# A gated-convolution and RG-LRU layer on one core: the 512-column moving operands of TensorE stored even columns first and read in pairs

## The chip, the cores and the metric

The kernel runs on one core of one Trainium2 chip. The metric is the device time of one execution in microseconds (us); lower is better. Before the change three timed runs gave 851.17, 851.32 and 853.02 us, a median of 851.32. The trace that is read here is a further execution that took 851.45 us; its first and last instruction lie 849.7 us apart (the span).

## The reference, cut to what matters

One layer acts on 512 latent tokens and 256 context tokens of width 2048, all in float32:

```
mod_lat = silu(c) @ w_ada + b_ada                 # shift, scale, gate; the same for c_ctx
hl = rmsnorm(x)   * (1 + scale_l) + shift_l       # 512 latent tokens
hc = rmsnorm(ctx) * (1 + scale_c) + shift_c       # 256 context tokens
b, c, u, g, v, q = split(h @ w_in)                # w_in: 2048 x 6144; context needs v alone
ya = b * conv3(c * u) * silu(g)                   # head group A
xb = conv4(v) + bias                              # head group B
a, bt = lru_coeffs(xb)                            # two directions, 16 block-diagonal heads
yb = (scan_fwd + scan_bwd) * silu(q)              # latent scans start from the context's state
out = x + gate_l * (concat(ya, yb) @ w_out)       # w_out: 2048 x 2048
return rmsnorm(out) * final_g
```

## The kernel before, in words

The host lays the inputs out: x is handed over transposed, as 16 tiles of 128 channels by 512 tokens (`xt`), w_in as tiles of 128 rows whose columns are the weights of one or several output tiles, w_out as 32 pieces of 128 rows by two times 512 columns (`wout`).

Large products run in float32r, one pass over the array, and three of them make one product of nearly float32 accuracy. Each operand is split into a high part, rounded to float32r by ScalarE, and a low part, the difference, by VectorE (`split`, lines 70 to 75; `make_h`, lines 250 to 254; `y_split`, lines 573 to 578). `mm3` (lines 77 to 80) then issues high times high, low times high and high times low into one accumulator in PSUM. In a matmul one operand is stationary: 128 columns of it are loaded into the array first. The other, the moving operand, streams through it column by column, here 512 at a time, or 256 for the context.

The work goes in three phases, and TensorE's instruction order is the order of the program text:

- Phase A (lines 222 to 346). Sums of squares over the 16 x tiles give rinvB, the inverse norm of each token, spread over the partitions. Then, for each of the 16 slices k of the 2048 channels: the adaLN products of that slice (`ada`, 64 small float32 matmuls of 64 columns by 32), the normalised latent tile h (`h_lat`), and seven output tiles of w_in (`main_a`), whose seven accumulators stay open over the whole loop. h is the moving operand, tokens along its columns.
- Phase B (lines 581 to 624). The other 41 output tiles of w_in come as 82 pieces of 1024 columns, each half of one tile's reduction: 8 slices, three matmuls of 512 latent columns each. The v tiles take the context's 256 columns too. Between the pieces run the convolutions, the gates and the RG-LRU of one of eight channel blocks at a time (`l_prep`, `l_gate`, `l_exp`, `l_mul`, `l_scan`), spread over steps by a table (`bg`, `mid`). VectorE also sums up the gate products of adaLN (`gt_acc`).
- Phase D (lines 680 to 734). The product with w_out, 8 pieces for each of four column blocks c of 512. Here the weights are the moving operand (lines 705 to 707), and the split y tiles, 128 tokens at a time, are stationary. Four token blocks t give four accumulators. VectorE adds the residual (`d_add`), ScalarE sums squares (`d_sq`), and `fin0` to `fin2` normalise and store. In the first three column blocks the adaLN gate is multiplied onto the product; in the last one (c == 3) `split_piece` (lines 314 to 321) multiplies it onto the 1024 raw weights before they are split.

Weights come through five raw buffers and three split ones. One DMA queue, SyncE's, issues all loads; a piece is loaded three steps and split two steps ahead of its use.

Nothing is computed along the columns of h before the matmuls that mixes them: the norm's square sums, rinvB and h keep whatever order of tokens x arrives in. The columns of PSUM that a matmul writes are in the order in which its moving columns are read.

Of the kernel before, what the change touches and what calls it, by code (L numbers as in the profile page):

```python
# [10 lines left out]
ALU = mybir.AluOpType  # L11
# [4 lines left out]
KT = D // 128  # L16
T = 512
# [26 lines left out]
N_D = 32  # L44
# [5 lines left out]
def tile_hybrid_layer(ctx, tc, xt, ct, xn, wada, wgt, bgt, wa_, wbc, wout, lruw, par, ident, fg, out):  # L50
    nc = tc.nc
# [8 lines left out]
    hl = s_lat.enter_context(p_lat)  # L60
# [9 lines left out]
    def split(raw, n=1024):  # L70
        hi = stage.tile([128, 1024], F32R, name="whi", bufs=3)
        lo = stage.tile([128, 1024], F32R, name="wlo", bufs=3)
        nc.scalar.copy(hi[:, :n], raw[:, :n])  # L73
        nc.vector.tensor_tensor(lo[:, :n], raw[:, :n], hi[:, :n].bitcast(F32), op=ALU.subtract)  # L74
        return hi, lo

    def mm3(acc, wh, wl, h, n, first, last, **kw):
        nc.tensor.matmul(acc, wh, h[0][:, :n], start=first, stop=False, **kw)  # L78
        nc.tensor.matmul(acc, wl, h[0][:, :n], start=False, stop=False, **kw)  # L79
        nc.tensor.matmul(acc, wh, h[1][:, :n], start=False, stop=last, **kw)  # L80


    pt = const.tile([128, NP], F32, name="pt")
# [7 lines left out]
    for k in range(KT):  # L91
        t = hl.tile([128, T], F32, name="xhi", bufs=17)
# [70 lines left out]
    acc = [pa.tile([128, 512], F32, name="bacc") for i in range(NA - 2)]  # L163
# [19 lines left out]
    gq = [None]  # L183
# [52 lines left out]
    for j in range(4):  # L236
        nc.tensor.matmul(acc[5][:, 2 * j:2 * j + 2], ssum[:, 128 * j:128 * j + 128], cmean[:, 0:2],
                         start=True, stop=True, skip_group_check=True)
# [57 lines left out]
    def main_a(k, j):  # L296
        hi, lo = wsp["a", k]
        s = slice(128 * j, 128 * j + 128)
        mm3(acc[j], hi[:, s], lo[:, s], hlat[k], T, k == 0, k == KT - 1)
# [9 lines left out]
    def load_piece(s):  # L309
        t = raw_tile()  # L310
        nc.sync.dma_start(t, piece_src(s))
        rawq[s] = t

    def split_piece(s):
        raw = rawq.pop(s)
        c = (s - N_BC) // 8
        if c == 3:
            r3 = raw.rearrange("p (k n) -> p k n", k=2)
            g = gq[0][:, None, 512 * c:512 * c + 512].to_broadcast([128, 2, 512])
            nc.vector.tensor_tensor(r3, r3, g, op=ALU.mult)  # L320
        wsp[s] = split(raw)

    h_lat(0)
# [193 lines left out]
    for m in range(NM):  # L517
        b = S_C0 + 7 * m
# [46 lines left out]
    accs = {}  # L565
# [7 lines left out]
    def y_split(pool, k):  # L573
        hi = pool.tile([128, T], F32R, name="yhi")
        lo = pool.tile([128, T], F32R, name="ylo")
        nc.scalar.copy(hi, y_src(k))
        nc.vector.tensor_tensor(lo, y_src(k), hi.bitcast(F32), op=ALU.subtract)
        yhl[k] = (hi, lo)

    load_piece(2)  # L580
    for s in range(N_BC):
        ti, half = divmod(s, 2)
        n, m = BC_TILES[ti]
# [8 lines left out]
        if s + 2 < NS:  # L592
            split_piece(s + 2)
        for _ in range(min(len(evq), 4 if s == 0 else 2)):
            evq.pop(0)()
        hi, lo = wsp.pop(s)
# [4 lines left out]
        for k in range(8):  # L601
# [3 lines left out]
            kk = 8 * half + k  # L605
            w = slice(128 * k, 128 * k + 128)
            mm3(accs[ti][0], hi[:, w], lo[:, w], hlat[kk], T, kk == 0, kk == KT - 1)
        if n == "v":
            for k in range(8):
                kk = 8 * half + k  # L610
                w = slice(128 * k, 128 * k + 128)
# [20 lines left out]
    def d_add(c, t, ps):  # L632
        s = slice(512 * c, 512 * c + 512)
        if c < 3:
            g = dr.tile([128, 512], F32, name="dg", bufs=1)
            nc.vector.tensor_tensor(g, gq[0][:, s], ps, op=ALU.mult)  # L636
            ps = g
        nc.vector.tensor_tensor(xr[t][:, s], xr[t][:, s], ps, op=ALU.add)

    def d_sq(c, t):  # L640
        s = slice(512 * c, 512 * c + 512)
        sqd = dr.tile([128, 512], F32, name="dsq", bufs=1)
        nc.scalar.activation(sqd, xr[t][:, s], AF.Square, accum_out=ss[:, t, c:c + 1])
        if c < 3:
            nc.gpsimd.tensor_tensor(xr[t][:, s], xr[t][:, s], fgb[:, s], op=ALU.mult)

    def d_ev(c, t, ps):
        d_add(c, t, ps)
        d_sq(c, t)
# [30 lines left out]
    for q in range(N_D):  # L680
        s = N_BC + q
        c, kp = divmod(q, 8)
        if s + 3 < NS:
            load_piece(s + 3)
        if s + 2 < NS:
            split_piece(s + 2)
        if kp == 0:
            if pend is not None:
                for t in range(2):
                    d_ev(pend[0], t, pend[1][t])  # L690
            accs = [pa.tile([128, 512], F32, name="bacc") for _ in range(2 if c == 1 else 4)]
            if c == 1:
                pp = pa.tile([128, 2, 512], F32, name="plru", bufs=1)
                accs += [pp[:, 0, :], pp[:, 1, :]]
        if q < 5:
            nc.sync.dma_start(*((xr[q], xn[q]) if q < 4 else (fgb, fg)))
        hi, lo = wsp.pop(s)

        def dmm(t, kp, hi, lo):
            for i in range(2):  # L700
                kk = 2 * kp + i
                yh, yl = yhl[kk]
                ts = slice(128 * t, 128 * t + 128)
                w = slice(512 * i, 512 * i + 512)
                nc.tensor.matmul(accs[t], yh[:, ts], hi[:, w], start=kk == 0, stop=False)  # L705
                nc.tensor.matmul(accs[t], yh[:, ts], lo[:, w], start=False, stop=False)  # L706
                nc.tensor.matmul(accs[t], yl[:, ts], hi[:, w], start=False, stop=kk == KT - 1)  # L707

        if c == 3 and kp >= 5:
            tailw[kp] = (hi, lo)  # L710
            if kp == 7:
                for t in range(4):
                    for kq in range(5, 8):
                        dmm(t, kq, *tailw[kq])
                    d_add(3, t, accs[t])
                    d_sq(3, t)
                    fin1(t)
                    fin2(t)
        else:
            for t in range(4):  # L720
                dmm(t, kp, hi, lo)
        if c == 0:
            for k in range(2 * kp + 6, 2 * kp + 8):
                if k < KT:
                    y_split(dp1[0] if k < 8 else dp, k)
        if pend is not None and kp < 2:
            d_ev(pend[0], kp + 2, pend[1][kp + 2])
            if kp == 1:
                pend = None
        if c == 3 and kp == 4:  # L730
            for t in range(4):
                fin0(t)
        if kp == 7:
            pend = (c, accs)


def _layout(np, x, c, ctx, c_ctx, norm_g, w_ada, b_ada, w_in, w_conv_a, w_conv_b, b_conv_b,
            lru_wa, lru_ba, lru_wx, lru_bx, lru_lambda, w_out, final_g):
    ca = np.ascontiguousarray
    a = {}  # L740
    a["xt"] = ca(x[0].T.reshape(KT, 128, T))
    a["ct"] = ca(ctx[0].T.reshape(KT, 128, TC))
    a["xn"] = ca(x[0].reshape(4, 128, D))
    w = w_ada[0]

    shp, scp, gtp = w[:, :D], w[:, D:2 * D], w[:, 2 * D:]
    g = np.stack([scp.reshape(2, 8, 128, KT, 4, 32), shp.reshape(2, 8, 128, KT, 4, 32)], axis=5)
    a["wada"] = ca(g.transpose(3, 0, 2, 1, 4, 5, 6).reshape(KT, 2, 128, 2048))
    a["wgt"] = ca(gtp.reshape(KT, 128, 2, 1024).transpose(0, 2, 1, 3).reshape(2 * KT, 128, 1024))
    a["bgt"] = ca(b_ada[0, 2 * D:].reshape(1, D))  # L750
    wi = w_in[0].reshape(KT, 128, 48, 128)
    a["wa_"] = ca(wi[:, :, [W_OFF[n] + m for n, m in A_TILES], :].reshape(KT, 128, NA * 128))
    wb = wi[:, :, [W_OFF[n] + m for n, m in BC_TILES], :].reshape(2, 8, 128, len(BC_TILES), 128)
    a["wbc"] = ca(wb.transpose(3, 0, 2, 1, 4).reshape(N_BC, 128, 1024))
    wo = w_out[0].reshape(8, 2, 128, 4, 512)
    a["wout"] = ca(wo.transpose(3, 0, 2, 1, 4).reshape(N_D, 128, 1024))

    wl = np.stack([lru_wa[0], lru_wx[0]], axis=3).reshape(2, NM, 2, 64, 128)
    wl = wl.transpose(1, 3, 0, 2, 4).reshape(NM, 64, 512)
    a["lruw"] = ca(np.concatenate([wl, wl], axis=1))  # L760
    col = lambda v: v.reshape(-1, 128).T
    gb = np.concatenate([lru_ba[0].reshape(2, NM, 2, 64), lru_bx[0].reshape(2, NM, 2, 64)], axis=3)
    parts = {
        "ng": col(norm_g[0]), "bsc": col(b_ada[0, D:2 * D]), "bsh": col(b_ada[0, :D]), "c": col(c[0]),
        "cc": col(c_ctx), "wca": w_conv_a[0].reshape(3, NM, 128).transpose(2, 1, 0).reshape(128, 24),
        "wcb": w_conv_b[0].reshape(4, NM, 128).transpose(2, 1, 0).reshape(128, 32), "bcb": col(b_conv_b[0]),
        "gb": gb.transpose(3, 1, 0, 2).reshape(128, 32),
        "lam": lru_lambda[0].reshape(2, NM, 128).transpose(2, 1, 0).reshape(128, 16),
    }
    a["par"] = ca(np.concatenate([parts[n] for n, _ in PCOLS], axis=1))  # L770
    a["ident"] = np.eye(128, dtype=np.float32)
    a["fg"] = ca(np.broadcast_to(final_g, (128, D)))
    return a
# [19 lines left out]
```

## Time and profile before

| | before |
|---|---|
| median of three timed runs | 851.32 us |
| profiled execution | 851.45 us |
| its span | 849.7 us |
| TensorE matmul busy | 825.0 us (97%) |
| weight loads busy (beside matmuls) | 678.4 us (80%) |
| VectorE, ScalarE, GpSimd busy | 478.5, 365.5, 89.3 us |
| mean granted TensorE clock | 0.995 of full speed |

In the rows, PE is TensorE's matmuls, PEld its weight loads, DVE VectorE, ACT ScalarE, POOL GpSimd, SP SyncE; L78 is line 78 of the kernel. A name such as `bacc<-xhi,whi` reads: written tile, then moving operand, then stationary operand. Matmuls are pipelined, and the length shown for one contains the time its last column needs to come out of the array; what one matmul costs in a stream is the distance from its start to the next one's. A float32 product that is not float32r appears as two records, one for each of its passes.

### The profile page before, as it was taken

Reading aid. Unit: us, or ns where it says so; the run is one execution under the profiler, and the core shown is the slowest. Engines: PE = TensorE matmul, PEld = TensorE weight load, DVE = VectorE, ACT = ScalarE, POOL = GpSimd, SP = SyncE. Lnnn points to the kernel's source line nnn. Section 1 sums busy time; section 2 is a strip of 40 time slices with the busy share of each in tenths; the row PEclk is TensorE's granted clock in tenths of the full one; section 3 lists DMA queues with packets and bytes.
Section 4 is the critical chain, followed back from the end, with each engine's and each line's share of the span. In section 5 each row is a group of like instructions: output and inputs, shape, how many; then the busy total and the mean of one; then the engine's idle time right before and its main releaser. Section 6 shows DMA issues by size and latency. Waiting matters only on the chain.

```text
span 849.7 us, 13489 instructions
## 1 busy us (share of the span) xinstructions
PE 825.0 (97%) x5712; PEld 678.4 (80%) x5712; DVE 478.5 (56%) x639; ACT 365.5 (43%) x454; POOL 89.3 (11%) x64
## 2 busy tenths in 40 slices
PE   7899999999999999999999999999999999999995
PEld 2687787888888888878888888887878888888784
DVE  3644344884653564585848566764556734243565
ACT  4322124541010125757584857565847522222334
POOL 0000004300000000202020202120202002020200
PEclk9999999999999999999999999999999999999998
DMA  9989996433333234342535353433224732323205
GB/s 343 417 337 358 335 373 206 150 103 121 100 100 100 81 106 160 121 163 100 185 98 164 120 186 103 161 124 115 88 93 147 289 100 87 112 76 123 75 0 198
DMA packets 36494, 136.31 MB, mean 160 GB/s; under 512 B 4049, under 2 KB 6353, under 8 KB 31697
## 3 DMA queue, kind: packets, MB, share of 16 engines
q1 hardware_dynamic: 36434, 135.45, 46.1%
q8 instruction: 45, 0.74, 0.4%
q14 instruction: 15, 0.12, 0.0%
HBM read 131.24 MB, written 4.19 MB: 159 GB/s over the span
## 4 chain that ended last, share of the span: by engine, by line
PE 90%; DVE 4%; DMA 2%; ACT 2%; issue 1%; POOL 0%; SPq 0%; ACTq 0%; DVEq 0%; POOLq 0%
PE bacc L78 21%; PE bacc L79 20%; PE bacc L80 20%; PE bacc L705 6%; PE bacc L707 6%; PE bacc L706 6%; PE bacc L208 4%; DMA xhi<-in_xt 1%; DMA rada<-in_wada 1%; PE plru L450 1%; PE plru L707 1%; PE plru L706 1%; PE plru L78 1%; PE plru L79 1%; PE plru L80 1%
## 5 line engine op out<-in xcount | busy, mean ns | idle before, releaser
L74 DVE TENSOR_TENSOR wlo<-raw,whi 128x1024 fp32r<-128x1024 f32 (+1 forms) x130 | 160.3, 1237 | 242.7 <-ACT whi L73 241.3
L78 PE MATMUL bacc<-xhi,whi 128*128 128x512 f32 x736 | 291.1, 395 | 2.9 <-issue 1.6
L79 PE MATMUL bacc<-xhi,wlo 128*128 128x512 f32 x736 | 287.8, 391 | 2.6 <-issue 2.0
L80 PE MATMUL bacc<-hlo,whi 128*128 128x512 f32 x736 | 287.7, 391 | 1.4 <-issue 1.4
L73 ACT CAST whi<-raw 128x1024 fp32r<-128x1024 f32 (+1 forms) x130 | 134.3, 1035 | 236.2 <-PE bacc L80 126.0
L78 PEld LDWEIGHTS bacc<-xhi,whi 128*128 128x128 f32 x736 | 138.5, 188 | 33.2 <-issue 2.1
L80 PEld LDWEIGHTS bacc<-hlo,whi 128*128 128x128 f32 x736 | 138.5, 188 | 32.0 <-issue 2.2
L79 PEld LDWEIGHTS bacc<-xhi,wlo 128*128 128x128 f32 x736 | 138.6, 188 | 31.2 <-issue 2.3
L705 PE MATMUL bacc<-whi,yhi 128*128 128x512 f32 x224 | 87.3, 390 | 0.3 <-DVE dg L636 0.3
L707 PE MATMUL bacc<-whi,ylo 128*128 128x512 f32 x224 | 87.2, 389 | 0.0
L706 PE MATMUL bacc<-wlo,yhi 128*128 128x512 f32 x224 | 87.1, 389 | 0.0
L460 POOL TENSOR_TENSOR li<-li,xb 128x768 f32<-128x768 f32 x16 | 30.9, 1933 | 395.6 <-ACT li L457 395.6
L705 PEld LDWEIGHTS bacc<-whi,yhi 128*128 128x128 f32 x224 | 42.0, 188 | 9.6 <-DVE dg L636 1.0
L456 ACT ACTIVATE lr<-plru,pt 64x768 f32<-64x768 f32 x32 | 28.7, 898 | 48.3 <-PE plru L453 41.3
L252 ACT ACTIVATE xhi<-xhi,sh 128x512 fp32r<-128x512 f32 x16 | 11.6, 724 | 87.9 <-DVE xhi L251 87.9
L706 PEld LDWEIGHTS bacc<-wlo,yhi 128*128 128x128 f32 x224 | 42.0, 188 | 8.7
L707 PEld LDWEIGHTS bacc<-whi,ylo 128*128 128x128 f32 x224 | 42.1, 188 | 8.7
L500 DVE SCALAR_TENSOR_TENSOR gacc<-raw,cs,gacc 128x1024 f32<-128x1024 f32 x32 | 42.5, 1328 | 0.1
L79 PE MATMUL bacc<-xchi,wlo 128*128 128x256 f32 x128 | 36.2, 283 | 0.0
L80 PE MATMUL bacc<-hclo,whi 128*128 128x256 f32 x128 | 36.2, 283 | 0.0
L78 PE MATMUL bacc<-xchi,whi 128*128 128x256 f32 x128 | 36.1, 282 | 0.0
L208 PEld LDWEIGHTS bacc<-rada,cs 128*32 128x32 f32 x2048 | 29.5, 110 | 6.7 <-issue 6.4
(158 smaller groups left out, 864.0 us busy)
## 6 DMA issues: line engine op xcount, KB each, us to landing
raw<-in_wbc SPq DMA_DIRECT2D x82, 512.0 KB, 3.5
rada<-in_wada SPq DMA_DIRECT2D x32, 1024.0 KB, 8.0
raw<-in_wgt SPq DMA_DIRECT2D x32, 512.0 KB, 4.4
raw<-in_wout SPq DMA_DIRECT2D x32, 512.0 KB, 3.5
raw<-in_wa_ SPq DMA_DIRECT2D x16, 448.0 KB, 9.4
xhi<-in_xt SPq DMA_DIRECT2D x16, 256.0 KB, 4.8
xr<-in_xn SPq DMA_DIRECT2D x4, 1024.0 KB, 4.9
xchi<-in_ct SPq DMA_DIRECT2D x16, 128.0 KB, 4.4
```

What stands on the lines that cost most here:

```text
L73: nc.scalar.copy(hi[:, :n], raw[:, :n])
L74: nc.vector.tensor_tensor(lo[:, :n], raw[:, :n], hi[:, :n].bitcast(F32), op=ALU.subtract)
L78: nc.tensor.matmul(acc, wh, h[0][:, :n], start=first, stop=False, **kw)
L79: nc.tensor.matmul(acc, wl, h[0][:, :n], start=False, stop=False, **kw)
L80: nc.tensor.matmul(acc, wh, h[1][:, :n], start=False, stop=last, **kw)
L208: nc.tensor.matmul(o[32 * q:32 * q + 32], cs[:, 8 * p + j, :], r[:, j, q, :], start=p + j == 0, stop=p + j == 8, skip_group_check=True)
L456: nc.scalar.activation(lru["r", d][o], pf[0:64, :TA], AF.Sigmoid, bias=b[0:64])
L460: nc.gpsimd.tensor_tensor(lru["i", d], lru["i", d], xb[m], op=ALU.mult)
L500: nc.vector.scalar_tensor_tensor(gacc[:, s], gtq.pop(i), cs[:, k, 0:1], gacc[:, s], op0=ALU.mult, op1=ALU.add)
L705: nc.tensor.matmul(accs[t], yh[:, ts], hi[:, w], start=kk == 0, stop=False)
L706: nc.tensor.matmul(accs[t], yh[:, ts], lo[:, w], start=False, stop=False)
L707: nc.tensor.matmul(accs[t], yl[:, ts], hi[:, w], start=False, stop=kk == KT - 1)
```

## The change

The host stores the 512 columns of every x tile, and of each 512-column half of a w_out piece, even columns first: 0, 2, 4, ..., 510, 1, 3, ..., 511. `pairs` gives the matmul a view of such an operand that reads one column of the first half, one of the second, and so on, which is the original order 0, 1, 2, 3, ... Consecutive columns that the matmul reads are thus 256 elements (1024 bytes) apart in SBUF, where they were adjacent. The results in PSUM have the order they had. The multiplication of the gate onto the last eight w_out pieces becomes two VectorE instructions of 512 columns, which read the gate with a step of two elements, in place of one of 1024. The context's matmuls of 256 columns, the adaLN products and the RG-LRU's gate products stay as they are.

```diff
--- before.py
+++ after.py
@@ -74,10 +74,15 @@
         nc.vector.tensor_tensor(lo[:, :n], raw[:, :n], hi[:, :n].bitcast(F32), op=ALU.subtract)
         return hi, lo
 
-    def mm3(acc, wh, wl, h, n, first, last, **kw):
-        nc.tensor.matmul(acc, wh, h[0][:, :n], start=first, stop=False, **kw)
-        nc.tensor.matmul(acc, wl, h[0][:, :n], start=False, stop=False, **kw)
-        nc.tensor.matmul(acc, wh, h[1][:, :n], start=False, stop=last, **kw)
+    def pairs(ap):
+
+        return ap.rearrange("p (a b) -> p b a", a=2)
+
+    def mm3(acc, wh, wl, h, n, first, last):
+        hh, hl = (pairs(t) if n == T else t[:, :n] for t in h)
+        nc.tensor.matmul(acc, wh, hh, start=first, stop=False)
+        nc.tensor.matmul(acc, wl, hh, start=False, stop=False)
+        nc.tensor.matmul(acc, wh, hl, start=False, stop=last)
 
 
     pt = const.tile([128, NP], F32, name="pt")
@@ -315,9 +320,10 @@
         raw = rawq.pop(s)
         c = (s - N_BC) // 8
         if c == 3:
-            r3 = raw.rearrange("p (k n) -> p k n", k=2)
-            g = gq[0][:, None, 512 * c:512 * c + 512].to_broadcast([128, 2, 512])
-            nc.vector.tensor_tensor(r3, r3, g, op=ALU.mult)
+            g = gq[0][:, 512 * c:512 * c + 512].rearrange("p (b a) -> p a b", a=2)
+            for r in (raw[:, :512], raw[:, 512:]):
+                r = r.rearrange("p (a b) -> p a b", a=2)
+                nc.vector.tensor_tensor(r, r, g, op=ALU.mult)
         wsp[s] = split(raw)
 
     h_lat(0)
@@ -702,9 +708,10 @@
                 yh, yl = yhl[kk]
                 ts = slice(128 * t, 128 * t + 128)
                 w = slice(512 * i, 512 * i + 512)
-                nc.tensor.matmul(accs[t], yh[:, ts], hi[:, w], start=kk == 0, stop=False)
-                nc.tensor.matmul(accs[t], yh[:, ts], lo[:, w], start=False, stop=False)
-                nc.tensor.matmul(accs[t], yl[:, ts], hi[:, w], start=False, stop=kk == KT - 1)
+                wh, wl = pairs(hi[:, w]), pairs(lo[:, w])
+                nc.tensor.matmul(accs[t], yh[:, ts], wh, start=kk == 0, stop=False)
+                nc.tensor.matmul(accs[t], yh[:, ts], wl, start=False, stop=False)
+                nc.tensor.matmul(accs[t], yl[:, ts], wh, start=False, stop=kk == KT - 1)
 
         if c == 3 and kp >= 5:
             tailw[kp] = (hi, lo)
@@ -738,7 +745,9 @@
             lru_wa, lru_ba, lru_wx, lru_bx, lru_lambda, w_out, final_g):
     ca = np.ascontiguousarray
     a = {}
-    a["xt"] = ca(x[0].T.reshape(KT, 128, T))
+
+    even = lambda v: ca(v.reshape(*v.shape[:-1], -1, 2).swapaxes(-1, -2)).reshape(v.shape)
+    a["xt"] = even(x[0].T.reshape(KT, 128, T))
     a["ct"] = ca(ctx[0].T.reshape(KT, 128, TC))
     a["xn"] = ca(x[0].reshape(4, 128, D))
     w = w_ada[0]
@@ -753,7 +762,7 @@
     wb = wi[:, :, [W_OFF[n] + m for n, m in BC_TILES], :].reshape(2, 8, 128, len(BC_TILES), 128)
     a["wbc"] = ca(wb.transpose(3, 0, 2, 1, 4).reshape(N_BC, 128, 1024))
     wo = w_out[0].reshape(8, 2, 128, 4, 512)
-    a["wout"] = ca(wo.transpose(3, 0, 2, 1, 4).reshape(N_D, 128, 1024))
+    a["wout"] = even(wo.transpose(3, 0, 2, 1, 4)).reshape(N_D, 128, 1024)
 
     wl = np.stack([lru_wa[0], lru_wx[0]], axis=3).reshape(2, NM, 2, 64, 128)
     wl = wl.transpose(1, 3, 0, 2, 4).reshape(NM, 64, 512)
```

## Rows read from the trace of the kernel before

**Rows 1.** The page: busy time by engine, granted clock in 40 slices, chain by engine

```profile
PE 825.0 (97%) x5712; PEld 678.4 (80%) x5712; DVE 478.5 (56%) x639; ACT 365.5 (43%) x454; POOL 89.3 (11%) x64
...
PEclk9999999999999999999999999999999999999998
...
PE 90%; DVE 4%; DMA 2%; ACT 2%; issue 1%; POOL 0%; SPq 0%; ACTq 0%; DVEq 0%; POOLq 0%
```

**Rows 2.** Groups by line, forms kept apart: names, shapes, xcount | busy us, mean ns

```profile
L78 PE MATMUL bacc<-xhi,whi 128*128 128x512 f32 x736 | 291.1, 395 | 2.9 <-issue 1.6 <-ACT whi L73 1.3
...
L705 PE MATMUL bacc<-whi,yhi 128*128 128x512 f32 x224 | 87.3, 390 | 0.3 <-DVE dg L636 0.3
...
L78 PE MATMUL plru<-xhi,whi 128*128 128x512 f32 x32 | 12.5, 389 | 0.0
...
L705 PE MATMUL plru<-whi,yhi 128*128 128x512 f32 x32 | 12.4, 389 | 0.0
```

**Rows 3.** Timeline of TensorE at the end of phase D: start us, length us, line, operation

```profile
831.62 0.39 PE L706 MATMUL bacc<-wlo,yhi 128*128 128x512 f32 x1
...
840.69 0.39 PE L707 MATMUL bacc<-whi,ylo 128*128 128x512 f32 x1
```

**Rows 4.** Timeline of TensorE in phase B, context columns of a v tile

```profile
282.00 0.28 PE L79 MATMUL bacc<-xchi,wlo 128*128 128x256 f32 x1
...
283.92 0.28 PE L80 MATMUL bacc<-hclo,whi 128*128 128x256 f32 x1
```

**Rows 5.** Timeline of TensorE in phase A, after a wait

```profile
38.96 0.59 PE L79 MATMUL bacc<-xhi,wlo 128*128 128x512 f32 x1 [1.96 <-issue]
...
39.77 0.63 PE L78 MATMUL bacc<-xhi,whi 128*128 128x512 f32 x1
...
41.48 0.63 PE L79 MATMUL bacc<-xhi,wlo 128*128 128x512 f32 x1
...
42.27 0.39 PE L78 MATMUL plru<-xhi,whi 128*128 128x512 f32 x1
```

**Rows 6.** Windows: us, busy of PE, PEld, DVE, ACT, POOL (xcount), PEclk, DMA, GB/s

```profile
39.00:42.00 3.00, 3.00 (x8) 2.32 (x8) 2.13 (x5) 1.55 (x2) 0.00 (x0) 0.50 1.03 424
...
580.00:583.00 3.00, 3.00 (x12) 1.79 (x11) 0.01 (x1) 1.10 (x2) 1.70 (x1) 1.00 0.87 273
```

**Rows 7.** Chain of waits, in order of time: start us, us, what

```profile
580.73 1.72 PE bacc L505 x4
```

**Rows 8.** TensorE's waits: waited for: us in total, times, longest us

```profile
PE bacc L79 <- issue: 2.0, 1, 2.0
PE plru L450 <- ACT li L457: 1.7, 2, 1.2
...
PE bacc L78 <- issue: 1.6, 1, 1.6
PE bacc L80 <- issue: 1.4, 1, 1.4
...
PE bacc L208 <- issue: 0.9, 1, 0.9
...
PE bacc L705 <- DVE dg L636: 0.3, 1, 0.3
```

**Rows 9.** VectorE's groups by line: columns as in rows 2

```profile
L636 DVE TENSOR_TENSOR dg<-gacc,bacc 128x512 f32<-128x512 f32 x10 | 6.8, 683 | 0.2
...
L153 DVE TENSOR_TENSOR w<-w,w 128x16 f32<-128x16 f32 x7 | 1.2, 175 | 0.2
...
L132 DVE TENSOR_TENSOR cs<-pt,sg 128x16 f32<-128x16 f32 x2 | 0.3, 184 | 2.1 <-ACT sg L130 2.1
```

**Rows 10.** Timeline of VectorE in phase D, between two w_out pieces

```profile
788.30 1.22 DVE L320 TENSOR_TENSOR raw<-raw,gacc 128x1024 f32<-128x1024 f32 x1
792.59 1.22 DVE L74 TENSOR_TENSOR wlo<-raw,whi 128x1024 fp32r<-128x1024 f32 x1 [3.08 <-ACT whi L73]
```

## The prediction

> **What bounds the kernel now.** I read the page first. TensorE is busy for 97% of the span, its granted clock reads 9 or more tenths in every slice but the last, and 90% of the chain that ended last runs over TensorE [rows 1]. So what one matmul costs in a stream decides, and VectorE (56%) and ScalarE (43%) lie beside it.
>
> The groups by line, forms kept apart, give the number of matmuls that the change touches [rows 2]. L78, L79 and L80 each have 736 of 512 columns into `bacc` and 32 into `plru`; L705, L706 and L707 have 224 and 32 each. That is 3 x 768 + 3 x 256 = 3072.
>
> The timeline gives their price. Between the starts at 831.62 and 840.69 lie 40 matmuls of 512 columns: 9.07 / 40 = 0.2267 us [rows 3]. Between 282.00 and 283.92 lie 16 of 256 columns: 0.120 us [rows 4]. The difference, 256 columns in 106.7 ns, is 2.4 columns per ns, one for each tick of the clock's upper level of 2.4 GHz. So 512 columns take 213.3 ns, and 13.3 ns per matmul are fixed. 3072 x 0.2267 = 696 us of the 849.7 us span are such matmuls.
>
> Two more rows say something on that fixed part. After a wait of 1.96 us the granted clock was 0.50 (the 1.2 GHz level), and the matmuls of 512 columns came every (41.48 - 39.77) / 4 = 0.4275 us [rows 5, 6]. That is 512 columns at 1.2 per ns (426.7 ns) with nothing fixed. And at a granted clock of 1.00 the four float32 passes of L505, also with 512 contiguous columns, took 1.72 us, 0.43 each [rows 6, 7]: two ticks per column, again with 3 ns left at most. The fixed 13.3 ns show only where a column is taken at each tick of 2.4 GHz. My reading, which no row proves: whatever brings the moving columns out of SBUF has no slack at that rate, and ample slack at half of it. Then anything that makes the bringing slower is paid in full.
>
> **The change part by part.** (1) In 3072 matmuls consecutive columns lie 1024 bytes apart, not 4. No row of TensorE shows a moving operand read in this way, so I bound it. The low end is below zero: the fixed 13.3 ns vanish, which would be -13.3 x 3072 = -40.9 us. For the high end the nearest row is on VectorE: L132 writes 16 elements 128 bytes apart in 184 ns, L153 writes 16 adjacent ones in 175 [rows 9], so 9 / 16 = 0.56 ns more per element. VectorE's own pace is (683 - 175) / (512 - 16) = 1.02 ns per column [rows 9], so a far element takes about 1.59 ns, 1.55 times a near one. Carried over as a time, 512 columns take 813 ns and a matmul 813 + 13.3 = 826: +600 ns, 3072 x 0.600 = +1842 us. Carried over as a factor, 213.3 x 1.55 = 331, and +117 ns each, +360 us.
>
> Between these I take one column per two ticks: two adjacent columns can come in one access, two far ones can't. Its row is TensorE's own half-rate stream, 427 to 430 ns for 512 columns [rows 5, 7]. A matmul then costs 426.7 + 13.3 = 440 ns, +213.3 ns, and 3072 x 0.2133 = +655.4 us. I keep the fixed part in it, since the reading would again be what is late; without it the sum would be 41 us less.
>
> [...]
>
> (2) What the added time hides. TensorE's waits in the loops are 2.0 + 1.7 + 1.6 + 1.4 + 0.9 + 0.3 = 7.9 us [rows 8]; they end with loads and with work on ScalarE and VectorE. With matmuls twice as long all these come early against TensorE, so the waits go. The stretch at half clock followed the longest of them; its seven matmuls at 0.43 in place of 0.23 us are another 1.4 us. Together -9.3 us. A lower clock, should the slower stream bring one, would cost little: at 1.2 GHz a column takes the 0.83 ns that it would cost anyhow [rows 5].
>
> (3) The gate on the last eight w_out pieces: one VectorE instruction of 1.22 us [rows 10] becomes two. By L636, which also multiplies 512 columns, they take 2 x 0.683 = 1.37 us [rows 9], 0.15 more; if the gate's step of two elements costs like the far elements of L132, 2 x (0.683 + 512 x 0.00056) = 1.94, 0.72 more. Per piece VectorE then sits idle for 3.08 us [rows 10], so 0.15 to 0.72 us is hidden, and more easily so if TensorE is slower. Without that cover it would be 1.2 to 5.8 us in all. I count 0.
>
> (4) Nothing else moves: the norms and h work on any order of tokens, PSUM gets the old order, and the loads have the same sizes. Weight loads, 80% busy [rows 1], lie under longer matmuls.
>
> Sum: the profiled execution took 851.45 us (849.7 of span and 1.75 around it; 0.13 above the median of 851.32). 851.45 + 655.4 - 9.3 = 1497.6, so **1498 us**.
>
> **The rivals.** [...]
>
> *The full price per column:* 1.59 ns, as worked out above; 851.45 + 1842 - 9.3 = 2684 us. For it: an access to another place has a time of its own, whatever the engine. Against it: L132 is a write of VectorE, and 9 ns between two small groups is a thin measure.
>
> *A partial price:* the factor of 1.55; 851.45 + 360 - 9.3 = 1202 us. For it is that same row; against it that it divides a fixed time by a slower engine's pace.
>
> *Faster:* two places in turn let the reading run ahead, and the fixed 13.3 ns hide as they do at half rate [rows 5, 7]. In phase A (16 x 7 x 3 = 336 matmuls) the DMA engines are full [rows 6], so I give it nothing there: 851.45 - 2736 x 0.0133 = 815 us. It decides as soon as the two halves are read at a column per tick. For it: nothing but that the 13.3 ns are not array time. Against it: if contiguous reading has no slack, scattered reading hardly gains some.
>
> **How the numbers follow.** Half rate 0.36 (1480 to 1525 by itself: the waits gone or not, VectorE hidden or not, some contention), no change 0.24, full price 0.17, partial 0.12, faster 0.08, and 0.03 for slower times in between. Faster by over 0.2%, about what can be told from no change here, is thus 0.08, the same 0.24, slower 0.36 + 0.17 + 0.12 + 0.03 = 0.68. The range takes in faster, no change, partial and half rate, 0.80: 812 to 1525. It leaves the full price out.
>
> **What would show it.** Starts of 512-column matmuls 0.44 us apart in phases B and D, and 0.120 us still for the context's 256 columns; TensorE's waits nearly gone, VectorE and ScalarE at about 32% and 24% of the span with unchanged busy times. L320's successor as two instructions of about 0.7 us. Starts still 0.227 apart mean no change; 0.21 to 0.22, faster; 0.34 or 0.83, the partial or full price. I am wrong if the distance does not move, which would mean that TensorE's reading doesn't depend on neighbours being adjacent.

## The result and the profile after

The change made the kernel faster: 831.03 us (median of four runs, 830.24 to 831.46) against 851.42 for the kernel before beside it, a ratio of 0.9756 (95% interval 0.9739 to 0.9772). I had forecast 1498. The profiled execution has a span of 829.3 us, 20.4 less than before.

The timeline of TensorE at the end of phase D (start us, length us, line, operation), to be held against [rows 3]:

```profile
811.02 0.38 PE L713 MATMUL bacc<-wlo,yhi 128*128 128x512 f32 x1
...
818.79 0.38 PE L713 MATMUL bacc<-wlo,yhi 128*128 128x512 f32 x1
...
820.30 0.38 PE L714 MATMUL bacc<-whi,ylo 128*128 128x512 f32 x1
```

From 811.02 to 818.79 lie 36 matmuls: 215.8 ns each, where [rows 3] gave 226.7. Of the 13.3 ns over the 213.3 of the columns 2.5 are left; 10.9 are gone. In the context's stretch of 256 columns, which the change leaves alone, the starts stay as far apart as in [rows 4]:

```profile
277.55 0.28 PE L84 MATMUL bacc<-xchi,wlo 128*128 128x256 f32 x1
...
279.93 0.28 PE L83 MATMUL bacc<-xchi,whi 128*128 128x256 f32 x1
```

That is 2.38 us for 20, 119 ns each. 3072 x 10.9 ns would be 33.5 us. The starts of the phases tell where 13 of them went. By line, the last adaLN product of phase A and the first and last matmul of phase D (duration min/median/max in ns, first and last start in us) are, in the kernel before:

```profile
L208 PE MATMUL bacc<-rada,cs x2048: 216/219/243, 19.2 to 133.9; 128*32 128x64 f32 x187
...
L705 PE MATMUL bacc<-whi,yhi x224: 389/389/497, 666.1 to 840.2; 128*128 128x512 f32 x112
```

and after:

```profile
L213 PE MATMUL bacc<-rada,cs x2048: 216/219/316, 19.3 to 134.3; 128*32 128x64 f32 x187
...
L712 PE MATMUL bacc<-whi,yhi x224: 379/379/484, 652.2 to 819.9; 128*128 128x512 f32 x112
```

| phase | matmuls of 512 | x 10.9 ns | measured | kept back |
|---|---|---|---|---|
| A (to the last adaLN product) | 336 | 3.7 us | -0.4 us | 4.1 |
| B (to the first of phase D) | 1968 | 21.5 us | 14.4 us | 7.1 |
| D | 768 | 8.4 us | 6.4 us | 2.0 |

Phase A is paced by its loads: between 30 and 120 us of the trace they move 357 GB/s before and after, and the DMA engines are busy 0.95 and 0.92 of that time; e4 below tests it. In phase B and D the waits of TensorE show what took the rest (waited for: us in total, times, longest us):

```profile
PE plru L456 <- ACT li L463: 7.6, 6, 2.5
...
PE bacc L713 <- DVE wlo L74: 0.8, 1, 0.8
...
PE bacc L712 <- DVE dg L642: 0.5, 1, 0.5
PE bacc L712 <- ACT whi L73: 0.4, 1, 0.4
```

The wait for the RG-LRU's gates (ACT li) was 1.7 us [rows 8] and is 7.6. After its longest, the timeline shows a second loss:

```profile
609.41 0.50 PE L456 MATMUL plru<-xs,lwh 128*128 128x512 f32 x1 [2.54 <-ACT li L463]
...
611.46 0.63 PE L83 MATMUL bacc<-xhi,whi 128*128 128x512 f32 x1
611.89 0.63 PE L84 MATMUL bacc<-xhi,wlo 128*128 128x512 f32 x1
```

Starts 0.43 us apart, twice the 215.8 ns, for eight matmuls: 1.7 us more; the granted clock is 0.50 between 611 and 613 us. With the 5.9 us of longer waits that makes 7.6, about the 7.1 that phase B kept back. What ScalarE waits for before it can write a gate is VectorE's sum of the last block's scans (xb), in the kernel before:

```profile
ACT li L457 <- DVE xb L488: 9.9, 7, 2.4
```

and after:

```profile
ACT li L463 <- DVE xb L494: 10.3, 7, 2.4
```

That wait hardly grew; TensorE now comes earlier to where it shows. Two windows (busy of PE, PEld, DVE, ACT, POOL, then granted clock and DMA), the first around the first such wait, show who is late:

```profile
350.00:364.00 14.00, 12.51 (x59) 10.62 (x57) 13.66 (x16) 6.08 (x7) 0.00 (x0) 1.00 0.33 112
...
609.00:613.00 4.00, 3.59 (x11) 2.96 (x12) 1.86 (x3) 3.79 (x5) 0.65 (x1) 0.66 0.40 146
```

In the second row the granted clock has fallen to a mean of 0.66 behind the 2.54 us wait. In the first VectorE works 13.66 of 14 us. It had been nearly in time for steps of 24 x 0.2267 = 5.4 us and is late for steps of 24 x 0.2158 = 5.2.

### The profile page after: what moved, and what is told of

The parts are those of the page before. It is cut to its first block, busy times and chain, and to the rows that moved or that the text cites. A ratio compares the mean times of both kernels' runs of the same rounds, so it can differ in the third digit from the quotient of the medians.

```text
span 829.3 us, 13497 instructions
## 1 busy us (share of the span) xinstructions
PE 796.2 (96%) x5712; PEld 683.0 (82%) x5712; DVE 483.1 (58%) x647; ACT 364.1 (44%) x454; POOL 90.4 (11%) x64
## 4 chain that ended last, share of the span: by engine, by line
PE 72%; DVE 14%; ACT 6%; issue 3%; DMA 2%; POOL 2%; SPq 0%; ACTq 0%; POOLq 0%; DVEq 0%
PE bacc L84 16%; PE bacc L83 16%; PE bacc L85 15%; PE bacc L713 5%; PE bacc L714 5%; PE bacc L712 5%; PE bacc L213 4%; DVE wlo L74 3%; ACT whi L73 2%; DVE li L493 1%; DVE lt L488 1%; DMA rada<-in_wada 1%; DMA xhi<-in_xt 1%; POOL sqc L283 1%; ACT li L463 1%
## 5 line engine op out<-in xcount | busy, mean ns | idle before, releaser
L83 PE MATMUL bacc<-xhi,whi 128*128 128x512 f32 x736 | 282.5, 384 | 3.3 <-issue 1.7
L84 PE MATMUL bacc<-xhi,wlo 128*128 128x512 f32 x736 | 281.4, 382 | 2.4 <-DVE wlo L74 1.3
L85 PE MATMUL bacc<-hlo,whi 128*128 128x512 f32 x736 | 279.8, 380 | 1.9 <-issue 1.9
L712 PE MATMUL bacc<-whi,yhi 128*128 128x512 f32 x224 | 85.2, 380 | 0.9 <-DVE dg L642 0.5
L713 PE MATMUL bacc<-wlo,yhi 128*128 128x512 f32 x224 | 85.0, 379 | 0.8 <-DVE wlo L74 0.8
L714 PE MATMUL bacc<-whi,ylo 128*128 128x512 f32 x224 | 84.9, 379 | 0.0
```

What stands on the lines that cost most here:

```text
L83: nc.tensor.matmul(acc, wh, hh, start=first, stop=False)
L84: nc.tensor.matmul(acc, wl, hh, start=False, stop=False)
L85: nc.tensor.matmul(acc, wh, hl, start=False, stop=last)
L712: nc.tensor.matmul(accs[t], yh[:, ts], wh, start=kk == 0, stop=False)
L713: nc.tensor.matmul(accs[t], yh[:, ts], wl, start=False, stop=False)
L714: nc.tensor.matmul(accs[t], yl[:, ts], wh, start=False, stop=kk == KT - 1)
```

## The experiments

**Streams of matmuls by themselves.** Three kernels leave the layer out and run streams of 40 matmuls on loaded tiles, one order of reading per stream. N is 40, W(i) the next of eight stationary tiles, and turn(x5, 2) the same view as `pairs`; every matmul loads its stationary operand anew:

```diff
+    # contig
+    for i in range(N):
+        nc.tensor.matmul(acc[0], W(i), x5, start=i == 0, stop=i == N - 1)
+    # halves
+    for i in range(N):
+        nc.tensor.matmul(acc[0], W(i), turn(x5, 2), start=i == 0, stop=i == N - 1)
+    ...   # other views of x5 = x[:, :512], other sizes, bfloat16 copies
```

Expected of the first: 

> Not the layer: twenty streams of 40 float32r (two of them bfloat16) matmuls, each reloading its stationary operand, that differ in the order in which the moving columns are read and in the sizes. Read is the distance from start to start. All theories: contiguous 512 columns 227 ns, two halves in turn 216 ns. Theory 'weights': the 13.3 ns are reads of the stationary operand that take turns from a contiguous moving stream, so they shrink with the stationary columns: contiguous 512 with 64 stationary columns 220 ns, with 32 217 ns; 256 contiguous 120, 256 halves 109. Theory 'restart': a fixed start of reading per matmul, whatever the stationary operand: 227 with 64 and 32 stationary columns too. Theory 'shape': a view of two dimensions is enough, so 216 for the view of two dimensions in contiguous order, 227 for the others only if their view is one-dimensional. On the order: if only leaving the 16 bytes of the last column counts, turns between columns 2 apart stay at 227 and those 4 or more apart give 216; four, eight and 32 places in turn 216 too if any scatter helps, 430 or more if two places is what can be held at once; a step of two columns 227 or more. bfloat16 216 both ways.

Expectation and result meet in its timeline, one row per stream (start, from first start to last end, number); the distance is the length less one matmul's, over the number less one:

```profile
22.94 9.23 PE L90 MATMUL acc<-x,w 128*128 128x512 f32 x40
...
32.01 8.80 PE L93 MATMUL acc<-x,w 128*128 128x512 f32 x40
...
49.73 9.23 PE L99 MATMUL acc<-x,w 128*128 128x512 f32 x40
...
58.79 8.80 PE L102 MATMUL acc<-x,w 128*128 128x512 f32 x40
...
93.33 11.49 PE L114 MATMUL acc<-x,w 128*128 128x512 f32 x40
...
124.11 17.10 PE L120 MATMUL acc<-x,w 128*128 128x512 f32 x39
...
141.45 17.79 PE L123 MATMUL acc<-x,w 128*128 128x512 f32 x39
...
204.54 19.05 PE L144 MATMUL acc<-xbf,wbf 128*128 128x512 bf16 x39
```

L90 is contiguous, (9.23 - 0.39) / 39 = 226.7 ns; L93 the halves in turn, (8.80 - 0.38) / 39 = 215.9: the layer's effect, without the layer. L99 takes turns between columns 2 apart (0, 2, 1, 3, ...), inside 16 bytes: nothing gained, 226.7. L102 takes turns between columns 4 apart: all gained, 215.9. L114, four places, 283; L120, 32 places, 433; L123, a step of two, 451; L144, bfloat16 in halves, 484. A view of two dimensions in contiguous order took 226.7, so it isn't the shape. Stationary operands of 64 and 32 columns gave 230 and 232, so a shorter weight load does not take the 13.3 ns away: 'weights', which had 220 and 217, and 'shape' fall. 'Restart', the 'fixed' of the next run, is nearest, but it had 227 for both. bfloat16 in halves, for which 216 was expected, is a miss.

Expected of the second: 

> Not the layer: streams of 40 float32r (three: bfloat16) matmuls again. Theory 'line': a contiguous run gets its next 16 bytes only every 1.77 ns (226.7 / 128; the step of two took 451 / 256 = 1.76), so time per matmul is the greater of columns / 2.4 + 2.5 ns and lines x 1.77: 384 contiguous 170, 384 halves 163; 256 contiguous with 64 stationary columns 113 to 115, halves 109; 256 columns with a step of two 227, with a step of four 453. Theory 'fixed': 13.3 ns per contiguous matmul of any length: 384 contiguous 173, 256 with 64 stationary columns 120. Both: 128 columns are bound by the weight load. Halves in turn in runs of 2, 4 and more: if what helps is that two lines are in flight, runs of 2 and 4 give 216 and long runs (64) 227; if single columns in turn are needed, all 227. Six places in turn 300 or more; four and eight places in neighbouring lines as four and eight places far apart (283, 487) if the number of places decides, less if the distance does. Start 8 bytes into a line 229 (one line more) or 227. Reversed 227. Halves 2 KB apart 216. Stationary operand with a step of two 227. bfloat16, which took 216 contiguous and 484 in halves: runs of 2 columns (4 bytes) from each half 216, turns within neighbouring 16 bytes 484 if the pair of 4 bytes decides.

384 contiguous columns took 173.7, as 'fixed' had it, and 256 with 64 stationary ones 113.3, as 'line' had it; 'line' also had 453 for 256 columns with a step of four, which took 233: neither holds. Missed by both were a start 8 bytes later (at column 2), reversed columns and a stationary step of two (233 each, where 227 or 229 were expected) and bfloat16 in runs of two (271, not 216). Its main surprise was the runs (halves in turn, but two columns from each, then four):

```profile
81.02 13.32 PE L117 MATMUL acc<-x,w 128*128 128x512 f32 x40
...
104.18 9.17 PE L123 MATMUL acc<-x,w 128*128 128x512 f32 x37
```

L117 is runs of two, 328 ns, L123 runs of eight, 243, both worse than contiguous, where 216 or 227 were expected. So turns between two places are not enough by themselves; single columns in turn make the gain (215.9). That suggested an account, 'two readers': the columns at even and at odd places of the order are fetched apart, each fetch keeping 16 bytes. No run shows readers or fetches. By the account each reader would use two columns of the same 16 bytes in contiguous order before it needs the next; in halves it would use four; in runs of two it would leave them at each column. By that count runs of two should cost what the step of two does, 451, and not 328, so the account gives at best the direction there.

Expected of the third: 

> Not the layer: streams of 40 float32r matmuls. Theory 'two readers': the columns at even and at odd places of the reading order are fetched separately, each fetch holds 16 bytes, and a fetch is free if it serves four columns of its own reader, just short if it serves two (contiguous), and twice too slow if it serves one. Rival 'two lines': what helps is that neighbours in the order lie in different 16 bytes, two places being kept. Each column read twice in a row (both readers walk through the same 16 bytes, four columns each): readers 216, lines 227. Halves with a step of two columns (two per line for each reader): readers 227 to 234, lines 216. Halves of 256 columns in all with a step of four (one per line): readers 214 or more, lines 112. One column 512 times 216 by both. Halves that start 8 bytes into a line: readers 216 (a line more per matmul). Stationary operand: if its loads are what the contiguous stream loses its ns to, the same stationary tile each time leaves 227, a step of four there raises it to 233 or more, and a halves stream stays at 216 with a stationary step of two. Contiguous 320, 448 and 480 columns: columns / 2.4 plus 6.7 or 13.3 ns in steps.

```profile
40.29 8.80 PE L96 MATMUL acc<-x,w 128*128 128x512 f32 x40
...
57.67 9.24 PE L102 MATMUL acc<-x,w 128*128 128x512 f32 x40
...
66.75 9.36 PE L105 MATMUL acc<-x,w 128*128 128x256 f32 x40
...
115.44 9.56 PE L123 MATMUL acc<-x,w 128*128 128x512 f32 x40
...
124.84 8.79 PE L126 MATMUL acc<-x,w 128*128 128x512 f32 x40
```

L96 reads each of 256 columns twice in a row, all neighbours within 16 bytes, and takes 215.8: 'two lines' had 227. L102, halves with a step of two, takes 226.7 and L105, 256 columns in halves with a step of four, 229.8, twice its 111.7 without the step: 'two lines' had 216 and 112. All three came out as 'two readers' had them. 448 and 480 contiguous columns were a miss: 16.0 and 16.7 ns over columns / 2.4, where 6.7 or 13.3 were expected. The last two rows vary the stationary operand: a step of four in it makes a contiguous stream slower, 235, and a step of two leaves the halves at 215.8, both as expected if a contiguous stream loses its ns to the reads of the stationary operand; no stream ran without those loads. The streams together, in ns from start to start, over the last 35:

| order of the moving columns, float32r | ns |
|---|---|
| 512 contiguous; in a view of two dimensions; 0, 2, 1, 3, ... | 226.7 |
| 512 contiguous from column 2 (8 bytes later); reversed | 233; 233 |
| two places in turn, 16 bytes to 2 KB apart; each column twice | 215.8 |
| halves with a step of two | 226.7 |
| halves in runs of 2, 4, 8, 16, 64 | 328, 250, 243, 240, 227 |
| one column 512 times | 218.6 |
| 4, 6 (504 columns), 8, 32 places in turn | 283, 291, 487, 433 |
| 4, 8 places, each 16 bytes from the next | 268, 480 |
| step of two; 256 columns with a step of two, of four | 451; 230, 233 |
| 480, 448, 384, 320 contiguous; 384 in halves | 216.7, 202.7, 173.7, 146.7; 162.5 |
| 512 contiguous: 64, 32 stationary columns | 230, 232 |
| 256 contiguous, in halves: 128 stationary columns | 120.0, 111.7 |
| the same: 64 stationary columns | 113.3, 109.1 |
| 128 contiguous, in halves: 128 stationary columns | 111.6, 111.7 |
| 512 contiguous, stationary step 2, step 4 | 233, 235 |
| bfloat16: contiguous or 0, 2, 1, 3; runs of 2; halves | 215.8; 271; 484 |

**One part of the change at a time.**

```diff
# e1: w_out as before
-                wh, wl = pairs(hi[:, w]), pairs(lo[:, w])
+                wh, wl = hi[:, w], lo[:, w]
...   # wout's layout and the gate's one instruction as before
# e2: x as before
-        hh, hl = (pairs(t) if n == T else t[:, :n] for t in h)
+        hh, hl = (t[:, :n] for t in h)
...   # xt's layout as before
```

> The change for the x tiles alone (phases A and B), w_out as before. If the gain is 10.9 ns per matmul less what waits give back, phase B alone gains about 14 us as in the trace of after, phase A nothing: 837 us. If phase A gained anything, less.

> The change for w_out alone (phase D), x as before: 768 x 10.9 = 8.4 us at most; the trace of after shows phase D 6.4 us shorter, so 845 us. The two parts add up to the whole change's -20.4 us if they don't touch each other.

837.37 us (ratio 0.9834, 0.9812 to 0.9856) and 844.88 (0.9926, 0.9909 to 0.9943), against 851.25. -13.9 and -6.4 make -20.3: the parts add up, -20.4 for the whole change.

**Phase A back to contiguous reading** (the columns of its seven tiles then stand in another order).

```diff
-        mm3(acc[j], hi[:, s], lo[:, s], hlat[k], T, k == 0, k == KT - 1)
+        mm3(acc[j], hi[:, s], lo[:, s], hlat[k], T, k == 0, k == KT - 1, lambda t: t)
...   # mm3 takes the view as an argument, pairs unless told otherwise
```

> The changed kernel with phase A's 336 matmuls reading the stored order as it lies (their columns then stand even first, so tiles of phase A mix up latent tokens; the time alone counts). If phase A is paced by its loads, nothing is lost: 831 us; if the faster matmuls of phase A count, 336 x 10.9 ns = 3.7 us slower, 834.7.

830.70 us (0.9751, 0.9735 to 0.9767): phase A's 336 faster matmuls are worth nothing, as they should be if its loads pace it.

**The context's tiles too.**

```diff
-        hh, hl = (pairs(t) if n == T else t[:, :n] for t in h)
+        hh, hl = (pairs(t[:, :n]) for t in h)
-    a["ct"] = ca(ctx[0].T.reshape(KT, 128, TC))
+    a["ct"] = even(ctx[0].T.reshape(KT, 128, TC))
```

> The changed kernel with the context's tiles stored and read in the same way: 384 matmuls of 256 columns at 112 in place of 120 ns, 3.2 us on a stretch without waits: 828 us (from 831.0). If weight loads hold the 256-column stream in the layer, 831.

827.12 us (0.9708, 0.9679 to 0.9737), 3.9 less than the change alone: as expected, within the spread of its runs (824.9 to 829.7).

**The lost third: the gates.**

```diff
# e5
-            at(b + 2 + i, l_gate, m, i // 2, i % 2, q=mid)
+            at(b + 2 + i, l_gate, m, i // 2, i % 2)
# e6, with e5; e7: both on the kernel before
-            lru["i", d] = lp[0].tile([128, TA], F32, name="li", bufs=2)
+            lru["i", d] = lp[0].tile([128, TA], F32, name="li", bufs=3)
```

> The changed kernel with the 32 gate products of the RG-LRU half a step later, at the end of a step of phase B rather than in its middle. If 8 of the lost us are TensorE's waits in L456 for ScalarE's last gate and the fall of the clock after the longest, most of them come back: 823 to 826 us. If VectorE's and ScalarE's work per step is itself too long, the waits only move: 829 to 832.

> The changed kernel with the gates half a step later and a third buffer for the gate tile li, so that a block's first gate does not wait for VectorE to have summed the scans of the block before. If that wait is where the 7.6 us go: 823 to 826 us, the waits of L456 under 2 us. If VectorE's queue as a whole is late in these steps: 829 to 831, with waits on wlo instead.

> The same two edits on the kernel before, whose steps are 5.4 us rather than 5.2. Its waits of L450 are 1.7 us in all, so 849.5 to 851.5 us; a gain of the size of the other run's would mean that the edits help by themselves and not by giving back what the faster matmuls lost.

e5: 830.56 us (0.9748, 0.9734 to 0.9763); the edit alone moved the waits (5.9 us for the gates, 3.1 for split weights) and gained nothing. e6: 828.54 (0.9732, 0.9717 to 0.9746), 2.5 less than the change alone and near the upper of its two forecasts. Its waits of TensorE:

```profile
PE bacc L84 <- DVE wlo L74: 7.1, 7, 1.6
...
PE plru L456 <- ACT li L463: 0.8, 1, 0.8
```

The gates no longer wait, but the split weights now come late from the same engine: the waits moved. e7: 852.01 (1.0011, 1.0000 to 1.0022): the edits are worth nothing at the old pace, and there too the waits only moved (3.2 us for split weights).

**All of it, and the gate sums moved.** e8 adds to e6 the context's tiles and stores the gate's last 512 columns even first on the host, so that VectorE multiplies each of the last eight pieces in one instruction again. e9 takes the 32 gate sums out of VectorE's full steps:

```diff
# e8, beside e3 and e6
-            g = gq[0][:, 512 * c:512 * c + 512].rearrange("p (b a) -> p a b", a=2)
-            for r in (raw[:, :512], raw[:, 512:]):
-                ...
+            r3 = raw.rearrange("p (k n) -> p k n", k=2)
+            g = gq[0][:, None, 512 * c:512 * c + 512].to_broadcast([128, 2, 512])
+            nc.vector.tensor_tensor(r3, r3, g, op=ALU.mult)
+    gtp[:, 1536:] = even(gtp[:, 1536:])   # host; the gate's bias likewise
# e9
-    for i in range(N_GT):
-        at(3 + 2 * i, gt_load, i)
-        at(4 + 2 * i, gt_acc, i)
+    gt_at = [*range(4, 22)] + [S_C0 + 7 * m + j for m in range(7) for j in (3, 5)]
+    for i, step in enumerate(gt_at):
+        at(step - 1, gt_load, i)
+        at(step, gt_acc, i)
...   # gt_sum after the last of them
```

> Changed kernel, context's tiles read in turn too (-3.9 us measured alone), gates late and li in three buffers, and the gate's last 512 columns stored even first by the host so that VectorE multiplies the last eight pieces in one instruction each, as before (phase D lost 2 of its 8.4 us after 805 us of the trace). If all hold: 818 to 822 us; if the gates' waits stay, 825 to 827.

> The kernel of e8 with the 32 gate sums of adaLN (1.33 us each on VectorE) taken out of the steps in which VectorE has a block's splits, its scans and a convolution to do: eighteen in the steps of the first tiles, two in lighter steps of each block. Theory 'queue': TensorE's 6.5 us of waits for wlo and the 2 us of clock and restarts behind them come from VectorE's queue being longer than a step there. Then most of them go: 816 to 820 us. Rival 'chain': the order of the block's own work sets them; 822 to 824.

e8: 823.28 us (0.9671, 0.9657 to 0.9686), between its two forecasts; the waits for wlo stay:

```profile
PE bacc L84 <- DVE wlo L74: 6.5, 6, 1.6
```

e9: **815.86 us** (0.9580, 0.9566 to 0.9595), slightly better than expected, the wait for the gates is gone and that for the split weights is down to:

```profile
PE bacc L84 <- DVE wlo L74: 1.0, 2, 0.6
```

So it was VectorE's queue in the steps with a block's splits and scans, not the order of the block's own work. This kernel beats both. The move of the gate sums was not run on the kernel before; there TensorE's waits for ScalarE and VectorE, outside the norm at the start, come to 3.9 us, so up to that much of what e9 gains over e8, 7.4 us, may not belong to the change.

**The order that I had priced.**

```diff
-        return ap.rearrange("p (a b) -> p b a", a=2)
+        return ap.rearrange("p (a b) -> p b a", a=32)
```

(and 32 for 2 in the host's layout and in the gate's view.)

> The changed kernel with 32 places in turn, 16 columns each, in place of two halves. If the price of the stream alone (433 ns) holds in the layer: 851 + 3072 x (0.433 - 0.227) less the waits that go, some 9 us: 1475 us, near the 1498 that was forecast for two places. If VectorE's and ScalarE's work hides some of it or the clock falls, 1400 or 1550.

1473.05 us in one run, as the stream's price had it; the timeline of TensorE shows starts 0.433 us apart, and the granted clock of the run is 0.996:

```profile
600.21 0.62 PE L84 MATMUL bacc<-xhi,wlo 128*128 128x512 f32 x1
600.65 0.61 PE L85 MATMUL bacc<-hlo,whi 128*128 128x512 f32 x1
601.08 0.62 PE L83 MATMUL bacc<-xhi,whi 128*128 128x512 f32 x1
```

## Why the prediction was wrong

**The step that failed** is in part (1): "Between these I take one column per two ticks: two adjacent columns can come in one access, two far ones can't." It made 440 ns of a matmul; the streams and the layer after show 215.8, less than the 226.7 of adjacent columns. That two adjacent columns come in one access was my assumption, and no run shows it. Some orders do cost about what I took: 32 places in turn (433 ns), a step of two (451), 8 places (487), bfloat16 in halves (484). Four places in turn cost 283 and runs of two 328, so one column per two ticks is no rule for columns that are far apart. That e10 comes near my forecast (1473 against 1498) is luck in part: 32 places were chosen when the stream had already given 433. The change's order is not scattered in this sense: each half is walked through column by column. I took "not adjacent" as the property that counts, where the times of several streams go with something else: how many columns in a row the even places of the order take from the same 16 bytes, and the odd places likewise.

**What was right.** The bound, the 3072 matmuls, and the 13.3 ns over the columns for the sizes in this layer; in contiguous streams of other sizes that part is 6.7 to 18 ns, so it is not fixed. The 2.4 and 1.2 GHz in the text are my reading: the rows show 2.4 columns per ns at a granted clock of 1.00, and 1.2 at 0.50. That contiguous reading of float32r has no slack at 2.4 columns per ns was a suspicion that the streams fit: a contiguous one got slower when the stationary operand was read with a step (226.7 to 233 and 235 for a step of two and four), and the halves stayed at 215.8 with a step of two. I drew the wrong conclusion from it, that any other order must be worse; the one that the change reads in is faster. The rival *faster* named what came, and its reason, that two places in turn let the reading run ahead, fits though no run shows it; it got 0.08. Against it I wrote "if contiguous reading has no slack, scattered reading hardly gains some", the same mistake.

**That rival's size**, 815 us, was 16 too low: 2.5 of the 13.3 ns per matmul stay (2736 x 2.5 ns = 6.8 us), and 9 us went into new waits of phases B and D and the clock behind one of them. That phase A gives nothing was right, and e4 shows it.

**Part (2)**, that waits go when matmuls get longer, was not tested by the change itself: matmuls got shorter and the waits grew. In e10, where they got longer, the sum holds with it: 851.45 + 3072 x (0.433 - 0.2267) - 9.3 = 1476, measured 1473. **Part (3)** was a little low:

```profile
L326 DVE TENSOR_TENSOR raw<-raw,gacc 128x512 f32<-128x512 f32 x16 | 14.9, 975 | 0.0
```

The pair of multiplications takes 2 x 0.975 = 1.95 us for the 1.22 of [rows 10] (the eight of the kernel before have a mean of 1.35), at the upper end that I gave. I counted 0, and some of it showed, since TensorE waited 0.8 us for the last split weights; in e8, with one instruction again, that wait is gone and phase D takes 175.4 us in place of 177.1, 8.1 less than before where 8.4 were to be had.

Whether neighbours in the order lie within the same 16 bytes does not sort the streams: in halves no two neighbours do, and that is the fast order, 215.8 ns. Counted for every second column by itself it fits in part: four uses of the same 16 bytes in a row give 215.8 ns, two 226.7, and one, with a step of two, 451. Runs of two and four places in turn have one use as well and take 328 and 283, and runs of 4 to 16 have two and take 250 to 240.

**What stays open.** That the order of reading alone makes the gain is shown; why it does is not. Two readers are an account which foretold three of the float32r streams and has the wrong price for others (runs of 2 to 16 columns, four places); no run looks inside. It does not say why a contiguous matmul loses 13.3 ns at 256, 320 and 512 columns, 13.7 at 384, 16.0 at 448 and 16.7 at 480, or 6.7 at 256 columns with 64 stationary ones, why 8 places are worse than 32, or why bfloat16 columns, which are as fast contiguous as float32r in halves, lose so much in halves (484). Whether a contiguous float32r stream is slow by itself, or only where its reads meet those of the stationary operand, is open: no matmul ran without a load of its own. The 111.7 ns of 256 columns in halves may be a floor of another kind, since 128 columns take as long (111.6 contiguous, 111.7 in halves).

## What to carry to other kernels

Where a stream of float32r matmuls runs start to start at columns / 2.4 plus 13 ns, store the moving operand so that single columns can be read in turn from two places at least 16 bytes apart: 5% of each matmul of 512 columns (226.7 to 215.8 ns), for a layout on the host and a view, as long as nothing else must know the order. Try an order of reading in a stream of 40 matmuls before pricing it; adjacency, steps and places each have their own price, and bfloat16 has the opposite sign (215.8 contiguous, 484 in halves). And before counting a gain of 5% on the bound engine, look which engines are just in time for a step: here about a third of the 33.5 us showed only when VectorE's work was cut down and spread.

## What the runs showed of the hardware

Of the orders in which 512 float32r columns were read, contiguous is not the fastest: 226.7 ns, against 215.8 in two places in turn, the time that bfloat16 takes contiguous; bfloat16 in two places in turn takes 484. A contiguous float32r stream gets slower with a step in the stationary operand (226.7, 233, 235 ns for a step of 1, 2, 4); in halves it stayed at 215.8 with a step of 2. A step of two costs a factor of two (451 for 512 columns), a step of four hardly more (for 256 columns 230 and 233), runs of two columns in halves 328, and 8 places, 487, more than 32, 433.
